# A state-space stage on a clock of TensorE time: eight heads' decay together, Silu on ScalarE, products in column halves

## The chip, the cores and the metric

The kernel runs on one core of one Trainium2 chip. A core has TensorE (PE, matrix products; its weight loads are listed apart as PEld), VectorE (DVE), ScalarE (ACT), GpSimd (POOL) and SyncE (SP, which here only issues transfers). Each engine executes its own list of instructions in order, and semaphores tie the lists together. The metric is device time in microseconds (us) of one execution. 2331.67 us is the median of three runs of the kernel before (2330.33 to 2332.08).

## The reference

Two layers over 256 tokens of width 2048 in float32. The first mixes tokens by attention, the second by a Mamba-2 state-space mixer; each is followed by a dense MLP, and all add to a residual stream. The state-space mixer, cut to what matters (h are the normalised tokens; 8 groups of 8 heads of 64; one chunk of 256 tokens, so the state carried in is zero):

```python
z, xbc, dt = jnp.split(h @ w_in, ...)                    # 4096 | 4096 + 1024 + 1024 | 64 columns
xbc = jax.nn.silu(causal_depthwise_conv(xbc, conv_w, conv_b))   # 4 taps along the tokens
xs, b_in, c_in = jnp.split(xbc, ...)
dt = jax.nn.softplus(dt + dt_bias)
cum = jnp.cumsum(dt * -jnp.exp(a_log))                   # running sum over the tokens
decay = jnp.exp(jnp.where(tril, cum[l] - cum[s], -inf))  # per head, 256 x 256
y = ((c_in @ b_in.T) * decay) @ (xs * dt) + d_skip * xs
y = rms_norm_per_group(y * jax.nn.silu(z)) * norm_g
return y @ w_out
```

## The kernel before, in words

The program is attention, MLP 0, the state-space stage, MLP 1. Float32 weights stream from memory over SP's queue into `wraw` (six buffers). ACT rounds each tile to a high part `wh` (L103), and DVE forms the low part `wl` (L104); each has four buffers, so a new `wh` waits until PE has used the one four units earlier. Such a tile holds two 128-row steps of a 512-column block. PE uses it in twelve matmuls of 128x512: for two steps and two halves of the tokens, activations high by weights high, low by high, and high by low (L326, L327, L330). I call these twelve a unit. The tiles' numbers run through the program; the stage begins with unit 421.

In the stage, a block of eight units projects one of B0, B1, C0, C1, x0 to x7, z0 to z7 (512 columns each) into two `acc` banks of PSUM. `evac` copies the banks to SBUF on ACT (L1090). For B, C and x, `conv` then works in two halves: four PE transposes (L1068), an Identity on ACT (L1074) and three taps on DVE (L1077) for each of two 128-channel tiles, then Silu as Tanh on ACT (L1079) and a product on DVE (L1080). The dt block gives 64 columns. `fold` (L354) turns them to tokens by heads, `dt_chain` computes softplus step by step on DVE (L1107 to L1123, `la` last), and `cums` (L1128, L1129) forms running sums on PE, which go to memory as `cumD` (L1131). `cb_group` makes a group's scores (L1153, L1154).

For an x block, `back` turns the result into tokens by channels (L1176, copied out at L1178), and `across` (L1190, L1192) adds what the first half of the tokens gives to the second. `head` works on one head: it reads its row of `cumD` into every partition (`cm`, L1210), subtracts and clamps on DVE (L1214), takes Exp on ACT (L1215), multiplies by dt and the scores on DVE (L1217), and multiplies on PE (`product`, L1226) into a bank of `yp`. The skip term and `far` are added on POOL and DVE (L1230 to L1233). `z_block` forms Silu of z from Tanh, and `gate` multiplies, normalises (L1264) and turns the result (L311) into operands of the output blocks o0 to o3, which use `acc` banks and end in a residual add on DVE (L396 or L421).

What sets the order: PE's order is the order in which the code issues its instructions. ACT, DVE, POOL and SP are ordered by a scheduler within what the data allows. In the code, small work is put off with `later(n, fn)`, which counts ticks, and a tick comes once in two units; `pump` issues one or two heads at every tick.

Of the kernel before, what the change touches and what calls it, by code (L numbers as in the profile page):

```python
# [43 lines left out]
C_INV, C_DTB, C_ALOG, C_CW, C_CB, C_END = 848, 880, 944, 1008, 1200, 1248  # L44
# [171 lines left out]
class Trunk:  # L216
# [120 lines left out]

    def narrow_block(self, key, tiles, then, lag=1):
# [203 lines left out]
    def mlp_body(self, mp, layer, gain):  # L542
# [47 lines left out]
        def products(accs, key, lhs, kt, first, last):  # L590
            u, (h, lo) = self.flow.next(key)
            for q in range(2):
                k = 2 * kt + q
                wh, wl = h[:, q * 512:(q + 1) * 512], lo[:, q * 512:(q + 1) * 512]
                for t, b in enumerate(accs):
                    ah, al = lhs(k, t)
                    nc.tensor.matmul(b, ah, wh, start=first and q == 0, stop=False)  # L597
                    nc.tensor.matmul(b, ah, wl, start=False, stop=False)  # L598
                    nc.tensor.matmul(b, al, wh, start=False, stop=last and q == 1)  # L599

# [36 lines left out]
        for tok in tokens:  # L637
            key = (tok[0], layer) + tok[1:]
            if tok[0] == "s":
# [8 lines left out]
                products([bank[name]], key, lambda k, t: [x[:, k] for x in S[name]], d,  # L648
# [4 lines left out]
            elif tok[0] == "c":  # L653
# [3 lines left out]
                products(out["c"], key, lhs_x, o, o == 0, o == 7)  # L657
# [8 lines left out]
            else:  # L666
# [3 lines left out]
                products(out[nb], key, lhs_u(p), o, o == 0, o == 3)  # L670
# [364 lines left out]
    def ssm_body(self, sp, dp, gain):  # L1035
        nc, d, cst = self.nc, self.d, self.cst
        xT = self.from_tiles(self.xT)
        rs, rsh = self.rs, self.rsh
        rs2 = self.rs_pool[(self.phase - 1) % 2][:, 0:2]
        tri = sp.tile([P, 256], F32, name="tri")  # L1040
        aneg = sp.tile([P, 64], F32, name="aneg")
        dt = sp.tile([P, 2, 64], F32, name="dt")
        ncum = sp.tile([P, 2, 64], F32, name="ncum")
        edge = sp.tile([P, 2, 64], F32, name="edge")
        cumD = dp.tile([64, S], F32, name="cumD")
        cb = [None] * GROUPS
        fm = {}
        xg = [None] * GROUPS
        yps = {}
        early = [True]  # L1050
        hq, ready, gated = [], set(), set()
        far = [None] * GROUPS

        def setup():
            nc.vector.tensor_copy(tri[:, 0:P], cst[:, C_TRI:C_TRI + P])
            nc.gpsimd.memset(tri[:, P:256], 1.0)
            nc.scalar.activation(aneg, cst[:, C_ALOG:C_ALOG + 64], AF.Exp)

        self.later(0, setup)

        def conv(ev, ct, dst, lag, after):

            def half(j):
                b = self.bank(early[0])
                for k in range(2):
                    for t in range(2):
                        o = k * 256 + t * P
                        nc.tensor.transpose(b[:, o:o + P], ev[t][:, (2 * j + k) * P:(2 * j + k + 1) * P], self.ident)  # L1068
                a = self.scratch()
                for k in range(2):  # L1070
                    c = ct + 2 * j + k
                    wc = lambda i: cst[:, C_CW + 4 * c + i:C_CW + 4 * c + i + 1]
                    s, o = b[:, k * 256:(k + 1) * 256], a[:, k * 256:(k + 1) * 256]
                    nc.scalar.activation(o, s, AF.Identity, bias=cst[:, C_CB + c:C_CB + c + 1], scale=wc(3))  # L1074
                    for i in (2, 1, 0):
                        m = 3 - i
                        nc.vector.scalar_tensor_tensor(o[:, m:256], s[:, 0:256 - m], wc(i), o[:, m:256], ALU.mult, ALU.add)  # L1077
                th = self.scratch()
                nc.scalar.activation(th, a, AF.Tanh, scale=0.5)  # L1079
                nc.vector.scalar_tensor_tensor(dst(j), th, 1.0, a, ALU.add, ALU.mult)  # L1080
# [427 lines left out]
```

## Time and profile before

| what | number |
|---|---|
| median of three runs | 2331.67 us (2330.33 to 2332.08) |
| the profiled execution | 2331.29 us; span of its instructions 2329.5 us |
| PE busy | 2312.2 us |
| DVE, ACT, POOL busy | 1905.8, 1385.4, 205.9 us |
| state-space stage, in the span's time | 961.48 to 1650.25 us |
| TensorE's granted clock | 1.00 |

The span runs from the first instruction to the last; 1.8 us of the execution lie around it. PE carries the time: a microsecond saved elsewhere counts only if PE waited for it. Matmuls overlap each other, so the time one costs is read from the distance between starts and not from its duration. In a row of groups the columns are line, engine, operation, tiles and shapes, count, busy us and mean ns, then the engine's idle time before the group and what ended it; in a timeline row start, busy time, engine, line, operation, tiles, shape and count.

### The profile page before, as it was taken

To read this page: it belongs to the slowest core of one execution; us is meant where nothing else is said; L and a number is where in the kernel's file an instruction comes from. 1 tells how busy PE (TensorE), PEld (TensorE's weight loads), DVE (VectorE), ACT (ScalarE), POOL (GpSimd) and SP (SyncE) were. 2 spreads that over 40 slices of the span, in tenths; PEclk is the share of its full clock that TensorE was granted. 3 is DMA by queue.
4 is the path that set the end of the run, shared out by engine and by line. 5 is a ranking of instruction groups with operands and counts; after the bars stand their busy time and mean duration, and the time that the engine had idled before them with its cause. 6 is when DMAs were issued, how large, how long until landed. Compare 5 with 4: busy or idle time off the path is not lost.

```text
span 2329.5 us, 30294 instructions
## 1 busy us (share of the span) xinstructions
PE 2312.2 (99%) x10799; PEld 1924.8 (83%) x10799; DVE 1905.8 (82%) x2432; ACT 1385.4 (59%) x1869; POOL 205.9 (9%) x239
## 2 busy tenths in 40 slices
PE   9999999999999999999999999999999999999999
PEld 7888888888888888888888888888888888888887
DVE  7776698998899897677788768666888899889885
ACT  6765566566566666555555455445566656666663
POOL 1431000000000000000022101110000000000000
PEclk9999999999999999999999999999999999999999
DMA  8434678878887877666566656656687788788874
GB/s 311 147 121 137 194 226 257 247 246 254 263 242 246 264 215 245 201 202 178 173 191 202 208 187 194 195 176 199 209 254 229 253 264 241 244 269 245 248 229 165
DMA packets 152152, 510.75 MB, mean 219 GB/s; under 512 B 17152, under 2 KB 26304, under 8 KB 152000
## 3 DMA queue, kind: packets, MB, share of 16 engines
q1 hardware_dynamic: 143712, 479.37, 62.6%
q0 software_dynamic: 8064, 29.36, 7.8%
q8 instruction: 85, 1.39, 0.2%
q14 instruction: 67, 0.55, 0.1%
q10 hardware_dynamic: 224, 0.07, 0.0%
HBM read 506.58 MB, written 2.16 MB: 218 GB/s over the span
## 4 chain that ended last, share of the span: by engine, by line
PE 97%; DVE 1%; DMA 1%; ACT 1%; issue 0%; POOL 0%; SPq 0%; DVEq 0%; ACTq 0%; POOLq 0%
PE acc L326 13%; PE acc L327 12%; PE acc L330 12%; PE yp L598 9%; PE yp L599 9%; PE yp L597 9%; PE st L598 8%; PE st L599 8%; PE st L597 8%; PE sm L311 2%; PE y L1226 1%; DVE wl L104 1%; PE acc L597 1%; PE acc L599 1%; PE acc L598 1%; PE acc L706 0%
## 5 line engine op out<-in xcount | busy, mean ns | idle before, releaser
L103 ACT ACTIVATE wh<-wraw 128x1024 fp32r<-128x1024 f32 (+2 forms) x818 | 860.0, 1054 | 633.2 <-PE acc L327 285.4
L104 DVE TENSOR_TENSOR wl<-wraw,wh 128x1024 fp32r<-128x1024 f32 (+2 forms) x818 | 995.3, 1229 | 253.4 <-ACT wh L103 243.7
L597 PE MATMUL yp<-wh,k 128*128 128x512 f32 x896 | 349.9, 390 | 0.0
L598 PE MATMUL yp<-wl,k 128*128 128x512 f32 x896 | 348.9, 389 | 0.6 <-DVE wl L104 0.6
L599 PE MATMUL yp<-wh,k 128*128 128x512 f32 x896 | 348.8, 389 | 0.0
L326 PE MATMUL acc<-wh,xt 128*128 128x512 f32 x704 | 280.5, 398 | 2.1 <-ACT wh L103 2.1
L327 PE MATMUL acc<-wh,xt 128*128 128x512 f32 x704 | 274.8, 390 | 0.0
L103 ACT ACTIVATE wh<-wrx 128x1024 fp32r<-128x1024 f32 x168 | 177.9, 1059 | 135.8 <-PE yp L599 107.5
L104 DVE TENSOR_TENSOR wl<-wrx,wh 128x1024 fp32r<-128x1024 f32 x168 | 203.8, 1218 | 38.2 <-ACT wh L103 38.0
L598 PEld LDWEIGHTS yp<-wl,k 128*128 128x128 f32 x896 | 168.2, 188 | 35.9 <-DVE wl L104 1.4
L326 PE MATMUL acc<-wh,k 128*128 128x512 f32 x496 | 196.8, 397 | 0.6 <-DVE xt L957 0.6
L599 PEld LDWEIGHTS yp<-wh,k 128*128 128x128 f32 x896 | 168.2, 188 | 35.0
L597 PEld LDWEIGHTS yp<-wh,k 128*128 128x128 f32 x896 | 168.2, 188 | 34.6
L327 PE MATMUL acc<-wh,k 128*128 128x512 f32 x496 | 193.4, 390 | 0.0
L330 PE MATMUL acc<-wl,xt 128*128 128x512 f32 x704 | 188.6, 390 | 0.0
L597 PE MATMUL st<-wh,xt 128*128 128x512 f32 x448 | 176.9, 395 | 0.0
L598 PE MATMUL st<-wl,xt 128*128 128x512 f32 x448 | 174.8, 390 | 0.0
L599 PE MATMUL st<-wh,xt 128*128 128x512 f32 x448 | 174.7, 390 | 0.0
L326 PEld LDWEIGHTS acc<-wh,xt 128*128 128x128 f32 x704 | 132.6, 188 | 29.8 <-ACT wh L103 3.7
L330 PEld LDWEIGHTS acc<-wl,xt 128*128 128x128 f32 x704 | 132.1, 188 | 28.2
L327 PEld LDWEIGHTS acc<-wh,xt 128*128 128x128 f32 x704 | 132.7, 188 | 25.9
L200 POOL DMA_DIRECT2D wrx<-mi x56 | 49.0, 875 | 1140.2 <-DVE wl L104 1034.2
(292 smaller groups left out, 3480.8 us busy)
## 6 DMA issues: line engine op xcount, KB each, us to landing
wraw<-mi SPq DMA_DIRECT2D x256, 512.0 KB, 5.1
wraw<-mo SPq DMA_DIRECT2D x256, 512.0 KB, 5.4
wraw<-si SPq DMA_DIRECT2D x160, 512.0 KB, 3.9
wraw<-so SPq DMA_DIRECT2D x64, 512.0 KB, 3.9
wrx<-mi SPq DMA_DIRECT2D x56, 512.0 KB, 5.0
wrx<-mi POOLq DMA_DIRECT2D x56, 512.0 KB, 7.8
wraw<-wo SPq DMA_DIRECT2D x32, 512.0 KB, 3.8
wraw<-ukv SPq DMA_DIRECT2D x16, 512.0 KB, 5.1
```

Source lines behind the costliest of these rows:

```text
L103: self.last = nc.scalar.activation(h[:, v], raw[:, v], AF.Copy)
L104: nc.vector.tensor_tensor(lo[:, v], raw[:, v], h[:, v].bitcast(F32), ALU.subtract)
L200: nc.gpsimd.dma_start(st["b11"].tile, quarter(d, 1, 0), accum_op=ALU.add)
L311: self.nc.tensor.transpose(b[:, j * P:(j + 1) * P], src[:, j * P:(j + 1) * P], self.ident)
L326: nc.tensor.matmul(accs[t][:, :n], ah, wh[:, q, :], start=first and kt + q == 0, stop=False)
L327: nc.tensor.matmul(accs[t][:, :n], al, wh[:, q, :], start=False, stop=False)
L330: nc.tensor.matmul(accs[t][:, :n], lhs(kt + q, t)[0], wl[:, q, :], start=False, stop=en and q == nk - 1)
L597: nc.tensor.matmul(b, ah, wh, start=first and q == 0, stop=False)
L598: nc.tensor.matmul(b, ah, wl, start=False, stop=False)
L599: nc.tensor.matmul(b, al, wh, start=False, stop=last and q == 1)
L1226: nc.tensor.matmul(y[t][:, o], half(t), xg[g][t][:, o], start=True, stop=True)
```

## The change

The stage is rewritten. PE's order now follows a clock (`at`): every unit moves it by 2.72 us, small runs add a fixed charge, and small work is issued when its planned time has come (`when`, `small`, `move`). Blocks come in another order: B0, dt, C0, x0, x1, B1, C1, z0, z1, x2, x3, o0 and so on. Silu is one ACT function in place of Tanh and a DVE product. The decay of a group's eight heads is made in four tiles of 128x512, each holding two heads: four reads of `cumD`, sixteen Relu rows, four Exp rows on ACT, four products with the scores on DVE; dt is multiplied into x (`xd`) instead. A group's product is one run of 32 matmuls, in which each 128x128 stationary tile is split into two halves of 64 columns that write different partitions of the same bank. The skip uses constants, on POOL. The output blocks o0 to o2 accumulate in the two `yp` banks (tiles `so`) instead of in `acc`, and y takes both banks of the pool `sm`, which the transposes and the across results use too. The three products of a weight tile are issued one after another for each bank (`products`).

```diff
-C_INV, C_DTB, C_ALOG, C_CW, C_CB, C_END = 848, 880, 944, 1008, 1200, 1248
+C_INV, C_DTB, C_ALOG, C_CW, C_CB, C_DSK, C_END = 848, 880, 944, 1008, 1200, 1248, 1312
...
+    def products(self, accs, key, lhs, kt, first, last):
+        nc = self.nc
+        u, (h, lo) = self.flow.next(key)
+        for q in range(2):
+            k = 2 * kt + q
+            wh, wl = h[:, q * 512:(q + 1) * 512], lo[:, q * 512:(q + 1) * 512]
+            for t, b in enumerate(accs):
+                ah, al = lhs(k, t)
+                nc.tensor.matmul(b, ah, wh, start=first and q == 0, stop=False)
+                nc.tensor.matmul(b, ah, wl, start=False, stop=False)
+                nc.tensor.matmul(b, al, wh, start=False, stop=last and q == 1)
...
+        at, due = [0.0, 0.0], []
+        count = [0]
+
+        def when(us, fn):
+            count[0] += 1
+            due.append((at[0] + us, count[0], fn))
+
+        def small(us, fn, gap=2.6):
+            at[1] = max(at[0] + us, at[1] + gap)
+            when(at[1] - at[0], fn)
+
+        def move(us):
+            at[0] += us
+            while due and min(due)[0] <= at[0]:
+                e = min(due)
+                due.remove(e)
+                e[2]()
+
...
-                th = self.scratch()
-                nc.scalar.activation(th, a, AF.Tanh, scale=0.5)
-                nc.vector.scalar_tensor_tensor(dst(j), th, 1.0, a, ALU.add, ALU.mult)
-            self.later(lag, lambda: half(0))
-            self.later(lag + 1, lambda: half(1))
-            if after:
-                self.later(lag + 5, after)
...
+                nc.scalar.activation(dst(j, a), a, AF.Silu)
+                if j:
+                    after()
+
+            small(2.5, lambda: half(0))
+            small(2.5, lambda: half(1), 4.0)
...
+            small(3, fold)
...
+                nc.tensor.matmul(b[:64, 0:P], la[:, 0], diagonal(), start=True, stop=True)
+                nc.tensor.matmul(b[:64, P:256], la[:, 0], ones[:, 0:P], start=True, stop=False)
+                nc.tensor.matmul(b[:64, P:256], la[:, 1], diagonal(), start=False, stop=True)
+                at[0] += 0.7
                 nc.scalar.activation(cum, b[:64, 0:256], AF.Copy)
+                nc.scalar.dma_start(cumD.rearrange("a (b s) -> (a b) s", b=2), cum)
+                small(2, back)
...
+            small(8, cums)
...
+            def back(t):
+                b = self.ps(self.sm, "sm")
+                for k in range(4):
+                    o = (k % 2) * 256 + t * P
+                    nc.tensor.transpose(b[:, k * P:(k + 1) * P], fmx[k // 2][:, o:o + P], self.ident)
+                at[0] += 0.45
+                x = sp.tile([P, 512], F32, tag="xtm", name=f"xtm{g}_{t}", bufs=XTM)
+                nc.scalar.activation(x, b, AF.Copy)
+                w = sp.tile([P, 512], F32, tag="xd", name=f"xd{g}_{t}", bufs=XD)
+                nc.vector.tensor_tensor(heads_of(w), heads_of(x), spread(dt[:, t], g), ALU.mult)
+                xg[g][t], xd[g][t] = x, w
+                if t == 0:
+                    xw = self.scratch()
+                    nc.gpsimd.tensor_tensor(heads_of(xw), heads_of(x), spread(edge[:, 0], g), ALU.mult)
+                    small(6, lambda: across(xw))
+                nc.gpsimd.tensor_tensor(heads_of(x), heads_of(x), spread(cst[:, C_DSK:C_DSK + 64], g), ALU.mult)
+                if t:
+                    waiting.append(g)
+                    if len(waiting) == 1:
+                        heads(g)
+
+            def across(xw):
+                b = self.ps(self.sm, "sm")
+                nc.tensor.matmul(b, cb[g][:, 2], xw, start=True, stop=True)
+                at[0] += 0.9
+                far = self.scratch()
+                nc.vector.tensor_tensor(heads_of(far), heads_of(b), spread(edge[:, 1], g), ALU.mult)
+                nc.gpsimd.tensor_tensor(xg[g][1], xg[g][1], far, ALU.add)
+
+            def after():
+                small(7, lambda: back(0))
+                small(7, lambda: back(1))
+
+            conv(ev, 4 * g, dst, after)
...
+        def heads(g):
+
+            cm = []
+            for i in range(4):
+                m = sp.tile([P, 2, 2, P], F32, tag="cm", name=f"cm{g}_{i}", bufs=4)
+                nc.sync.dma_start(m.rearrange("p a t n -> p (a t n)"), cumD[4 * g + i:4 * g + i + 1].to_broadcast([P, 2 * S]))
+                cm.append(m)
+
+            def exponent(i):
+                for k in range(2):
+                    for t in range(2):
+                        h = 8 * g + 2 * i + k
+                        nc.scalar.activation(cm[i][:, k, t], cm[i][:, k, t], AF.Relu, bias=cumT[:, t, h:h + 1], scale=-1.0)
+
+            def decay():
+                for m in cm:
+                    nc.scalar.activation(m, m, AF.Exp, scale=-1.0)
+                scores = cb[g][:, 0:2].rearrange("p t n -> p (t n)").unsqueeze(1).to_broadcast([P, 2, 2 * P])
+                for m in cm:
+                    v = m.rearrange("p a t n -> p a (t n)")
+                    nc.vector.tensor_tensor(v, v, scores, ALU.mult)
+                small(8, product)
+
+            def product():
+                y = [self.ps(self.sm, "y") for t in range(2)]
                 for t in range(2):
+                    for i in range(8):
+                        o = slice(i * 64, (i + 1) * 64)
+                        for r in (slice(0, 64), slice(64, 128)):
+                            nc.tensor.matmul(y[t][r, o], cm[i // 2][:, i % 2, t, r], xd[g][t][:, o], start=True, stop=True)
+                at[0] += 1.8
+                at[1] = max(at[1], at[0])
+                for t in range(2):
+                    nc.vector.tensor_tensor(xg[g][t], xg[g][t], y[t], ALU.add)
+                waiting.pop(0)
+                if waiting:
+                    heads(waiting[0])
+
+                def done():
+                    ready.add(g)
+                    gate(g)
+
+                when(2, done)
+
+            for i in range(4):
+                when(3 + 2.2 * i, lambda i=i: exponent(i))
+            when(11, decay)
...
-            m = sp.tile([P, 256], F32, tag="mt", name=f"mt{h}", bufs=6)
-            half = lambda t: m[:, t * P:(t + 1) * P]
-                nc.vector.tensor_scalar(half(t), cm[:, t * P:(t + 1) * P], ncum[:, t, h:h + 1], 0.0, ALU.add, ALU.min)
-            nc.scalar.activation(m, m, AF.Exp)
-                nc.vector.scalar_tensor_tensor(half(t), half(t), dt[:, t, h:h + 1], cb[g][:, 256 * t:256 * t + P],
-                                               ALU.mult, ALU.mult)
-                    nc.tensor.matmul(y[t][:, o], half(t), xg[g][t][:, o], start=True, stop=True)
-                if i == 7:
-                    for t in range(2):
-                        x = xg[g][t]
-                        nc.gpsimd.tensor_tensor(x, x, dg, ALU.mult)
-                        if t:
-                            nc.gpsimd.tensor_tensor(x, x, far[g], ALU.add)
-                        nc.vector.scalar_tensor_tensor(x, x, 0.5, y[t], ALU.mult, ALU.add)
-                    ready.add(g)
...
+                nc.scalar.activation(w, accs[t], AF.Silu, scale=rs[t])
...
+            small(10, lambda: turn(0))
+            small(10, lambda: turn(1))
+            small(12, lambda: gated.add(g))
...
+                    out = [self.ps(self.yp, "so") for _ in range(2)]
+                self.products(out, ("so", i, nb, o), self.from_tiles(yT_of(yT, i)), o, o == 0, o == 3)
+                if o == 3:
+                    self.add_residual(nb, out)
+                move(2.72)
...
+                self.products(accs, ("si", name, i, o), lhs_x, o, o == 0, o == 7)
+                if o % 2:
+                    self.tick()
+                if o == 7:
+                    done[name](i, accs)
+                move(2.72)
...
-SSM_ORDER = ["x0", "x1", "x2", "z0", "x3", "z1", "x4", "z2", "o0", "x5", "z3", "x6", "z4", "o1",
-             "x7", "z5", "z6", "o2a", "z7", "o2b", "o3"]
+SSM_ORDER = ["B0", "dt0", "C0", "x0", "x1", "B1", "C1", "z0", "z1", "x2", "x3", "o0", "z2", "z3", "x4", "x5", "o1",
+             "z4", "z5", "x6", "x7", "o201", "z6", "z7", "o223"]
```

PE at the end of the block x0, where its transposes stand (`s2` is a scratch tile that an evacuation wrote, `cst` holds the identity). Before (x0's transposes are the four that write `yp_737`):

```order
L330 MATMUL acc_735_9772<-wl463_9728,xt_636_8409 128x512
L330 MATMUL acc_736_9773<-wl463_9728,xt_636_8409 128x512
L1068 MATMUL yp_737_9810<-cst_90,s2_733_9768 128x128
L1068 MATMUL yp_737_9810<-cst_90,s2_734_9770 128x128
L1068 MATMUL yp_737_9810<-cst_90,s2_733_9768 128x128
L1068 MATMUL yp_737_9810<-cst_90,s2_734_9770 128x128
L326 MATMUL acc_735_9772<-wh464_9745,xt_647_8511 128x512
```

and now, units 445 and 446 (`acc_705`, `acc_706` are x0's banks):

```order
L347 MATMUL acc_705_9209<-wl445_9301,xt_669_8715 128x512
L348 MATMUL acc_705_9209<-wh445_9300,xt_670_8716 128x512
L346 MATMUL acc_706_9210<-wh445_9300,xt_669_8715 128x512
L347 MATMUL acc_706_9210<-wl445_9301,xt_669_8715 128x512
L348 MATMUL acc_706_9210<-wh445_9300,xt_670_8716 128x512
L1083 MATMUL sm_715_9402<-cst_90,s2_713_9398 128x128
L1083 MATMUL sm_715_9402<-cst_90,s2_714_9400 128x128
L1083 MATMUL sm_715_9402<-cst_90,s2_713_9398 128x128
L1083 MATMUL sm_715_9402<-cst_90,s2_714_9400 128x128
L346 MATMUL acc_717_9417<-wh446_9325,xt_636_8409 128x512
```

Before, the transposes stood behind the second unit (463) of the next block; now they stand directly behind the last unit of x0, which the evacuations read.

ACT around Silu of an x block's second half and the copies of its transposes back (`xtm`). Before, for x0, whose second Tanh (into `s2_743`) stands seven rows ahead of these, with x1's first half in between:

```order
L103 ACTIVATE wh474_9994<-wraw474_9925 128x1024
L103 ACTIVATE wh475_10030<-wraw475_9943 128x1024
L1074 ACTIVATE s2_752_10015<-sm_751_10010,cst_90 128x256
L103 ACTIVATE wh476_10048<-wraw476_9974 128x1024
L1074 ACTIVATE s2_752_10015<-sm_751_10010,cst_90 128x256
L103 ACTIVATE wh477_10118<-wraw477_9992 128x1024
L1079 ACTIVATE s2_753_10024<-s2_752_10015 128x512
L1178 ACTIVATE xtm0_0_10069<-sm_755_10064 128x512
L1178 ACTIVATE xtm0_1_10076<-sm_756_10071 128x512
```

and now, in x1, whose first transposes back stand on PE behind unit 457:

```order
L103 ACTIVATE wh459_9711<-wraw459_9590 128x1024
L1094 ACTIVATE s2_729_9630<-s2_729_9630 128x512
L1090 ACTIVATE s2_733_9669<-sm_732_9664,cst_90 128x256
L103 ACTIVATE wh460_9729<-wraw460_9642 128x1024
L103 ACTIVATE wh461_9759<-wraw461_9683 128x1024
L1094 ACTIVATE s2_733_9669<-s2_733_9669 128x512
L1214 ACTIVATE xtm1_0_9750<-sm_734_9745 128x512
```

The Silu of the second half (`s2_733`) now stands behind `wh461`, which reuses the buffer of `wh457`, and the transposes back that need it stand right behind unit 457; before, six units' `wh` stood between x0's second Tanh and the copies `xtm0_0`, `xtm0_1`.

DVE at the end of the dt chain. Before:

```order
L104 TENSOR_TENSOR wl438_9132<-wraw438_9075,wh438_9131 128x1024
L1117 SCALAR_TENSOR_TENSOR dt4_9051<-dt4_9051,dt3_9050 128x128 x4
L104 TENSOR_TENSOR wl439_9150<-wraw439_9093,wh439_9149 128x1024
L1117 SCALAR_TENSOR_TENSOR dt4_9051<-dt4_9051,dt3_9050 128x128 x3
L1118 SCALAR_TENSOR_TENSOR dt4_9051<-dt4_9051,dt2_9049 128x128
L1120 SCALAR_TENSOR_TENSOR dt_8757<-dt4_9051,dt0_9047 128x128
L1123 SCALAR_TENSOR_TENSOR la_9071<-dt_8757,aneg_8756 128x64 x2
L104 TENSOR_TENSOR wl440_9168<-wraw440_9111,wh440_9167 128x1024
```

and now, with `s2_694` and `s2_695` as scratch tiles of the chain and `la` in the last row:

```order
L1162 SCALAR_TENSOR_TENSOR s2_694_9020<-s2_694_9020 128x128
L104 TENSOR_TENSOR wl436_9086<-wraw436_8999,wh436_9085 128x1024
L1162 SCALAR_TENSOR_TENSOR s2_694_9020<-s2_694_9020 128x128
L104 TENSOR_TENSOR wl437_9110<-wraw437_9047,wh437_9109 128x1024
L1162 SCALAR_TENSOR_TENSOR s2_694_9020<-s2_694_9020 128x128
L1163 SCALAR_TENSOR_TENSOR s2_694_9020<-s2_694_9020,s2_695_9023 128x128
L1165 SCALAR_TENSOR_TENSOR dt_8755<-s2_694_9020 128x128
L1167 SCALAR_TENSOR_TENSOR s2_695_9023<-dt_8755,s2_695_9023 128x64 x2
```

The chain now shares DVE with a `wl` at each step, the last of them `wl437`; on PE the running sums stand behind unit 433.

More of the change, by code (lines that the diff above doesn't have):

```diff
@@ L1036, in ssm_body @@
         nc, d, cst = self.nc, self.d, self.cst
[L1037 to L1041, printed above, removed]
+        lhs_x = self.from_tiles(self.xT)
+        xT, rs = self.xT, self.rs
         dt = sp.tile([P, 2, 64], F32, name="dt")
-        ncum = sp.tile([P, 2, 64], F32, name="ncum")
+        cumT = sp.tile([P, 2, 64], F32, name="cumT")
@@ L1044, in ssm_body @@
         edge = sp.tile([P, 2, 64], F32, name="edge")
[L1045 to L1057, printed above, removed]
@@ new lines, in cb_group @@
+        def cb_group(g):
+            B, C = fm["B", g // 4][:, g % 4], fm["C", g // 4][:, g % 4]
+            b = self.ps(self.sm, "sm")
+            nc.tensor.matmul(b[:, 0:256], B[:, 0:P], C, start=True, stop=True)
+            nc.tensor.matmul(b[:, 256:384], B[:, P:256], C[:, P:256], start=True, stop=True)
+            at[0] += 0.65
+            t = sp.tile([P, 3, P], F32, name=f"cb{g}")
+            for i in range(2):
+                nc.vector.tensor_tensor(t[:, i], b[:, 2 * i * P:2 * i * P + P], diagonal(), ALU.mult)
+            nc.scalar.activation(t[:, 2], b[:, P:256], AF.Copy)
+            cb[g] = t
@@ new lines, in dt_products, with fold @@
+        def dt_products():
+            w = [t.rearrange("p (k n) -> p k n", n=P) for t in self.flow.next(("si", "dt", 0, 0))[1]]
+            acc = self.ps(self.sm, "sm")
+            for kt in range(16):
+                for i in range(2):
+                    nc.tensor.matmul(acc[:, :256], w[kt // 8][:, kt % 8], xT[kt // 4][i][:, kt % 4],
+                                     start=kt == 0 and i == 0, stop=kt == 15 and i == 1)
+            v = self.scratch()
+            nc.vector.tensor_copy(v[:, :256], acc[:, :256])
+            def fold():
+                b = self.ps(self.sm, "sm")
+                for t in range(2):
+                    nc.tensor.matmul(b[:, t * 64:(t + 1) * 64], v[:, t * P:(t + 1) * P], cst[:, C_SEL:C_SEL + 64],
+                                     start=True, stop=True)
+                dt_chain(b)
+            small(3, fold)
@@ L1104, in dt_chain @@
         def dt_chain(b):
-            v, e, s, z, q = (sp.tile([P, 2, 64], F32, name=f"dt{i}") for i in range(5))
+            work = self.scratch()
+            v, e, z, q = (work[:, i * P:(i + 1) * P].rearrange("p (t h) -> p t h", t=2) for i in range(4))
             for t in range(2):
@@ new lines, in ssm_body @@
+        while due:
+            assert at[0] < 1e6
+            move(max(0.0, min(due)[0] - at[0]))
+        assert len(gated) == GROUPS
+        self.boundary_begin(gain, True)
+        for pair in ((0, 1), (2, 3)):
+            accs = {}
+            for nb in pair:
+                accs[nb] = self.block([("so", 6, nb)], self.from_tiles(yT_of(yT, 3)), last=False)
+            for nb in pair:
+                self.block([("so", 7, nb)], self.from_tiles([yT[7]]), accs=accs[nb], first=False)
+                self.finalize(nb, accs[nb], False)
@@ L1488 @@
     a["sng"] = rows(f(ssm_norm_g)[0], 512)
-    a["dsk"] = rows(np.repeat(f(ssm_d)[0], 64), 512)
     one = np.ones((P, P), np.float32)
```

297 lines of the change are left out of this document (118 added, 179 removed).

## The prediction

> **What bounds the kernel now.** I read the page's table of engines first, then the state-space stage alone (from the first projection matmul to the last of o3's), then the waits of TensorE (PE).
>
> ```profile
> span 2329.5 us, 30294 instructions
> ...
> PE 2312.2 (99%) x10799; PEld 1924.8 (83%) x10799; DVE 1905.8 (82%) x2432; ACT 1385.4 (59%) x1869; POOL 205.9 (9%) x239
> ...
> 961.48:1650.25 688.77, 687.76 (x3294) 571.62 (x3292) 509.53 (x822) 362.84 (x503) 84.16 (x68) 1.00 0.62 192
> ...
> PE sm L1068 <- ACT xtm L1178: 0.5, 1, 0.5
> ...
> PE sm L1176 <- DVE s L1077: 0.2, 1, 0.2
> ```
>
> PE is busy 99% of the span. In the stage it is busy 687.76 of 688.77 us (second and third number of the row; then PE's weight loads, DVE, ACT, POOL, the clock at 1.00 and the DMA). So it stands idle for 1.0 us, and its small matmuls wait twice. VectorE (DVE, 509.53) and ScalarE (ACT, 362.84) have room. Only two things can move the time: less work on PE, or new waits in PE's fixed order. A faster helper engine alone buys 1.0 us at most.
>
> What PE's small runs cost is the distance between starts:
>
> ```profile
> 1110.93 1.07 PE L330 MATMUL acc<-wl,xt 128*128 128x512 f32 x4
> 1111.84 0.60 PE L1068 MATMUL sm<-cst,s 128*128 128x128 f32 x4
> 1112.19 0.48 PE L326 MATMUL acc<-wh,xt 128*128 128x512 f32 x1
> 1112.51 0.39 PE L327 MATMUL acc<-wh,xt 128*128 128x512 f32 x1
> ...
> 1132.12 1.02 PE L1190 MATMUL sm<-s,cb 128*128 128x512 f32 x2
> 1132.98 1.00 PE L1226 MATMUL y<-xtm,mt 128*128 128x64 f32 x8
> 1133.79 0.48 PE L326 MATMUL acc<-wh,xt 128*128 128x512 f32 x1
> 1134.11 0.39 PE L327 MATMUL acc<-wh,xt 128*128 128x512 f32 x1
> ...
> L1226 PE MATMUL y<-xtm,mt 128*128 128x64 f32 x256 | 33.5, 264 | 0.0
> ```
>
> Four big matmuls take 0.91 us from start to start (1110.93 to 1111.84), so 0.227 us each and 2.72 for a weight unit of twelve. A matmul runs 0.39 us, so it ends 0.16 us after its slot. Four transposes put 0.35 us in front of the next matmul and 0.09 behind it (0.32 to the next start instead of 0.23): 0.44. Two heads' products, 8 records, cost 0.81 + 0.09 = 0.90. The 256 records are 32 such pairs: 28.7 us.
>
> **The change, part by part.** Column halves first. Now 64 records stand together per group, each with 64 stationary columns and a 64-wide stream. No row shows two column tiles at work. The nearest is the running sums, which use one tile of 64 columns:
>
> ```profile
> 994.31 0.56 PE L354 MATMUL sm<-cst,s 128*128 128x64 f32 x4
> ...
> 1010.23 1.07 PE L330 MATMUL acc<-wl,xt 128*128 128x512 f32 x4
> 1011.22 0.65 PE L1128 MATMUL sm<-tri,la 128*64 128x256 f32 x2
> 1011.71 0.38 PE L1129 MATMUL sm<-tri,la 128*64 128x128 f32 x2
> 1012.02 0.50 PE L326 MATMUL acc<-wh,xt 128*128 128x512 f32 x1
> ...
> 1011.22 0.19 PEld L1128 LDWEIGHTS sm<-tri,la 128*64 128x64 f32 x2 [0.35 <-issue]
> 1011.49 0.35 PEld L1129 LDWEIGHTS sm<-tri,la 128*64 128x64 f32 x2
> ```
>
> After 1010.23 the next start was due 0.91 later, at 1011.14; it came at 1011.22, so entering and leaving the 64-column form costs about 0.2 us together. A record of the old product takes 0.101 us (0.81 over 8). With half the columns I put 0.056, half of the same spacing with its surcharge (0.90 over 8 is 0.112). One after the other, 64 records take 3.6 + 0.2 = 3.8 us a group: 30.4 in all, a loss of 1.7. If both halves work at once, 1.8 + 0.2 = 2.0: 16 in all, a gain of 12.7. If loads did not hide behind matmuls, 64 x 0.11 + 0.2 = 7.2: 57.6, a loss of 28.9. I take 2.0, at six to four against 3.8: the halves write different partitions and hold their own weights. The clock in the code charges 1.8 here, and its other charges (0.45 for four transposes, 0.9 across) agree with the rows (0.44; 1132.12 to 1132.98).
>
> On this row bears a rule against the change: the Trainium skill, "TensorE: Matmul & The Clock Gate", Part 3, says that a weight load overlaps matmuls in flight only when its row group differs. Both halves use all rows, so by it the sum would take 57.6. The trace disagrees: L1129's loads began at 1011.49, while L1128's matmuls ran to 1011.87, in the same rows. The same skill's "TensorEngine Tiling (Array Packing)", Tiling Modes, has different tiles load and multiply in parallel, which gives the 16; no run here shows it yet.
>
> Next, PE's waits. The clock in `move` runs small work at a planned time, but a block's last unit is charged only after its evacuation was booked, so `small(2.5)` lands directly behind that unit. PE executes in order and stands there. Prices:
>
> ```profile
> L1090 ACT ACTIVATE s<-acc,rs 128x512 f32<-128x512 f32 x24 | 15.0, 674 | 0.0
> L103 ACT ACTIVATE wh<-wraw 128x1024 fp32r<-128x1024 f32 x225 | 238.3, 1060 | 255.6 <-PE acc L327 210.8 <-issue 24.8 <-DVE mt L1214 6.9
> L1079 ACT ACTIVATE s<-s 128x512 f32<-128x512 f32 x24 | 15.1, 631 | 4.7 <-DVE s L1077 4.1
> ...
> L104 DVE TENSOR_TENSOR wl<-wraw,wh 128x1024 fp32r<-128x1024 f32 x225 | 282.8, 1261 | 128.1 <-ACT wh L103 126.8
> L421 DVE TENSOR_TENSOR x<-acc,x 128x512 f32<-128x512 f32 x24 | 15.4, 684 | 9.1 <-PE acc L330 9.1
> L1117 DVE SCALAR_TENSOR_TENSOR dt<-dt,dt 128x128 f32<-128x128 f32 x7 | 2.0, 289 | 0.2
> L1123 DVE SCALAR_TENSOR_TENSOR la<-dt,aneg 128x64 f32<-128x64 f32 x2 | 0.4, 222 | 0.0
> ...
> 1112.48 0.57 ACT L1074 ACTIVATE s<-sm,cst 128x256 f32<-128x256 f32 x1 [0.24 <-PE sm L1068]
> ...
> 1012.53 0.37 ACT L1130 ACTIVATE cum<-sm 64x256 f32<-64x256 f32 x1
> 1012.93 0.50 ACTq L1131 DMA_DIRECT2D cumD<-cum  x1
> 1017.37 0.81 SPq L1210 DMA_DIRECT2D cm<-cumD  x2
> ...
> L1109 ACT ACTIVATE dt<-dt 128x128 f32<-128x128 f32 x1 | 0.3, 288 | 0.0
> ...
> DMA to landing us min/median/max: 2.9/3.6/4.9
> ```
>
> From PE's end to ACT's start is 0.04 us (1111.84 + 0.60 to 1112.48); back to PE I put 0.05.
>
> 1. *Transposes behind a block's end.* The second bank's evacuation starts 0.16 + 0.04 after the unit and takes 0.67, plus 0.05: 0.92. The first bank's transpose runs in the first 0.1 of it, so 0.82 is lost, at six blocks (B0, x0, C1, x2, x4, x6): 4.9. B1 is a little later (1.0). In x1, x3, x5, x7 the across matmul stands ahead and covers all but 0.1: 0.4. At C0, ACT has twelve Relu rows and two wh ahead of the second evacuation, and the Relus wait for the running sums' round trip: copy 0.4, write 4.4 (1012.93 to the first read at 1017.37), read 3.6, Relus of 0.2 to 0.29 each, 2 x 1.06, 2 x 0.67 are 14.3 to 15.3 us after the sums, and C0 ends 11.3 after them (four units and a small run): 3 to 4, I take 3.0, since such rows overlap. Sum 9.3.
> 2. *Running sums.* `la` stands on DVE behind wl437, that behind wh437, which reuses the buffer of unit 433, the unit just finished: 0.2 + 1.06 + 1.26 + three DVE steps of 0.29 + two of 0.22 + 0.05 = 3.9, say 4.0. Before, 17 us of other matmuls lay between fold and sums (994.31 to 1011.22).
> 3. *B0's second half* wants the bank that DVE's copy of the dt product empties: 0.7.
> 4. *Odd x groups (x1, x3, x5, x7), first transposes back.* The second Silu stands on ACT behind the wh that reuses the buffer of the unit just finished: 0.2 + 1.06 + 0.63 + 0.05 = 1.9, less 0.2 for the two transposes that can go: 1.75 x 4 = 7.0.
> 5. *Across behind the product (same groups).* Its bank is y's of the even group, freed by a DVE add that stands behind a wl, behind a wh, behind the last big matmul: 0.2 + 1.06 + 1.26 + 0.68 = 3.2 against 2.0 of product: 1.15 x 4 = 4.6. With the product at 3.8 this is nothing.
> 6. *o blocks.* They accumulate in two banks of `yp` instead of four of `acc`, so a new column block waits for the residual add. The add of the first bank can start 0.5 before the unit ends and takes 0.68: 0.26; with one wl ahead about 0.6. At five places (two in o0, two in o1, one in o2): 2.9; the others fall under case 4.
>
> Sum of the waits: 9.3 + 4.0 + 0.7 + 7.0 + 4.6 + 2.9 = 28.5 us. The 1.0 us of old idle time goes.
>
> At nothing I cost what has cover. DVE loses the per-head work (L1214, L1217) and Tanh's second half. ACT gets 17 more table loads, 1.28 us each (22 us), and 128 Relu rows of 0.29 at most (37):
>
> ```profile
> L438 ACT ACT_TABLE_LOAD x1 | 1.3, 1283 | 1.2 <-PEq L1501 1.2
> ...
> L1214 DVE TENSOR_SCALAR mt<-cm,ncum 128x128 f32<-128x128 f32 x128 | 37.8, 338 | 0.0
> L1217 DVE SCALAR_TENSOR_TENSOR mt<-mt,dt,cb 128x128 f32<-128x128 f32 x128 | 39.5, 349 | 2.6 <-ACT mt L1215 2.3
> ```
>
> ACT then has some 420 of 700 us. A wh is made three units (8.2 us) ahead of its use, so two table loads in its way stay hidden; without that lead each would cost 1.3. The skip moves to POOL, off PE's path; gate chains get three units and need about 7 us. On SP's queue the four reads of a group's decay tiles now wait for the previous product, and weights stand behind them, but the next weight needs a buffer that frees no earlier: nothing.
>
> Sum: 2331.29 - 12.7 - 1.0 + 28.5 = 2346.1 us. The profiled execution (span 2329.5 plus 1.8 around it) is 0.4 below the median of the runs, 2331.67; that is inside the 0.2% (5 us) which I take as no change. I say 2346.
>
> **The rivals.**
> - *Halves one after the other* (0.25). The running sums' loads of one tile speak for it. Product -12.7 becomes +1.7, case 5 vanishes: 2331.3 + 1.7 - 1.0 + 23.9 = 2356.
> - *Loads not hidden* (0.05): the product adds 28.9, case 5 vanishes: 2331.3 + 28.9 - 1.0 + 23.9 = 2383. The overlap at 1011.49 speaks against it.
> - *Faster* (0.18): the other side. The halves overlap, and ACT and DVE take their ready short rows in time, so that PE's waits stay under the 13.7 us that the product and the old idle time give. The place is cases 2, 4 and 5, where the rows stand behind a wh that needs the unit just done. It decides at 13.7 us, about half of my waits; at a third (9.5) the time is 2327. Against it: engines run their rows in order in this trace (PE stood 0.49 us at L1068 for L1178), and the rows do stand so.
> - *No net change* (0.10): waits of 9 to 18 us, 2327 to 2336.
>
> **How the numbers follow.** My forecast (0.42) gives 2346, and 2339 to 2352 by case 1 at C0 and case 6 between their floors (0.8 and 0.26) and twice their price, with half a microsecond of lateness at each long wait. The range reaches down into the faster rival, 2326, and up past the serial one with the same lateness, 2362. Below lies most of the faster case, above the unhidden loads. Faster by over 0.2%: 0.18; within 0.2%: 0.10; slower: 0.72.
>
> **What would show it.** In the profile after: records of the product 28 ns apart (or 56, or 110); a wait of PE's transposes for the evacuation, about 0.8 us a dozen times in all; one of about 4 us for `la`; four near 1.75 for Silu; four near 1.1 for the y add; PE idle near 28 us where it was 1.0. I am wrong if PE's idle time in the stage stays under 14 us, or if the products take 3.8 a group.

## The result, and the profile after

The changed kernel takes 2353.9 us (median of four runs, 2352.72 to 2357.35) against 2331.43: 22.5 us more, a ratio of 1.0098 [1.0086, 1.011]. Its profiled execution took 2352.72 us. The head of its page, and the stage as a stretch of time (us, then busy us and instructions of PE, its weight loads, DVE, ACT, POOL, then clock, DMA share and GB/s):

```profile
span 2350.9 us, 30618 instructions
```

```profile
960.99:1671.17 710.18, 684.69 (x3551) 558.95 (x3550) 449.23 (x565) 410.55 (x617) 75.38 (x69) 1.00 0.58 183
```

PE's waits in the stage (what waited, for what; total us, times, longest):

```profile
PE sm L1083 <- ACT s L1072: 5.8, 11, 1.8
PE sm L1211 <- ACT s L1094: 5.8, 4, 1.4
...
PE sm L1175 <- DVE s L1167: 4.5, 1, 4.5
PE sm L1230 <- DVE xtm L1275: 4.3, 4, 1.1
PE so L346 <- DVE x L433: 4.0, 4, 1.7
...
PE sm L1083 <- DVE s L1133: 0.5, 1, 0.5
```

The span grew by 21.4 us, and so did the stage (710.18 against 688.77): the rest of the span kept its length to 0.1 us. PE now stands idle for 25.5 us of it (710.18 less 684.69) where it was 1.0, and the six waits listed, 24.9 us, are nearly all of that. L1083 are the transposes behind a block, L1211 the transposes back, L1175 the running sums, L1230 the across matmul, L346 into `so` the first matmul of an output column block.

The product of a group (timeline: start, busy us, engine, line, operation, tiles, shape, count):

```profile
1118.85 0.39 PE L348 MATMUL acc<-wh,xt 128*128 128x512 f32 x1
1119.17 2.08 PE L1271 MATMUL y<-xd,cm 128*64 128x64 f32 x64
1121.19 0.50 PE L346 MATMUL acc<-wh,xt 128*128 128x512 f32 x1
1121.52 0.39 PE L347 MATMUL acc<-wl,xt 128*128 128x512 f32 x1
```

The 64 records follow each other in 2.02 us (1119.17 to 1121.19), 32 ns each, where a full record took 101 before and the prediction put 56 for halves one after the other. The two halves work at once. With 0.09 in front (1118.85 + 0.23 to 1119.17) and 0.10 behind (0.33 to the next start) a group costs 2.2 us, all eight 17.7 instead of 28.7.

The longest wait, and what it did to the clock. First the rows around it:

```profile
1001.15 0.39 PE L348 MATMUL acc<-wh,xt 128*128 128x512 f32 x1
1001.57 1.06 ACT L103 ACTIVATE wh<-wraw 128x1024 fp32r<-128x1024 f32 x1 [0.24 <-PE acc L348]
...
1002.26 1.22 DVE L104 TENSOR_TENSOR wl<-wraw,wh 128x1024 fp32r<-128x1024 f32 x1
1003.40 0.28 DVE L1162 SCALAR_TENSOR_TENSOR s<-s 128x128 f32<-128x128 f32 x1
1003.60 1.22 DVE L104 TENSOR_TENSOR wl<-wraw,wh 128x1024 fp32r<-128x1024 f32 x1
1004.74 0.28 DVE L1162 SCALAR_TENSOR_TENSOR s<-s 128x128 f32<-128x128 f32 x1
...
1005.71 0.36 DVE L1167 SCALAR_TENSOR_TENSOR s<-dt,s 128x64 f32<-128x64 f32 x2
1005.99 0.69 PE L1175 MATMUL sm<-cst,s 128*64 128x128 f32 x2 [4.45 <-DVE s L1167]
...
1009.76 0.63 PE L348 MATMUL acc<-wh,xt 128*128 128x512 f32 x1
1010.18 0.63 PE L346 MATMUL acc<-wh,xt 128*128 128x512 f32 x1
```

and stretches of time, with PE's busy time as the second number and the granted clock as the third from the end:

```profile
1002.00:1005.00 3.00, 0.00 (x0) 0.00 (x0) 3.00 (x6) 0.63 (x1) 0.00 (x0) 1.00 0.82 259
1005.00:1012.00 7.00, 6.01 (x17) 4.78 (x18) 0.97 (x5) 0.38 (x1) 0.00 (x0) 0.51 0.58 197
1012.00:1014.00 2.00, 2.00 (x12) 1.39 (x11) 0.81 (x4) 1.45 (x2) 0.00 (x0) 1.00 0.73 158
```

The rows that were predicted are there: the last big matmul ends, ScalarE (ACT) rounds the weights of unit 437 (1001.57 to 1002.63), VectorE (DVE) makes their low part (1003.60) and only then the last steps of `la`. But DVE did not wait for this rounding. It was still making the low part of the unit before (1002.26), and the row of 1002 to 1005 has it busy for 3.00 of 3.00 us; its list has no gap from 996.6 until `la` is done. So the length of DVE's own list set the wait, and not the buffer that the unit just ended gave free. Then PE runs at half clock until 1012: big matmuls start 0.42 us apart instead of 0.227. Some 6 us of work at half speed lose 3 us.

The sum of 21.4 us: idle time +24.5; about 25 waits in which the first 0.16 us still count as busy, since the matmul before them is draining, +4.0; half clock +3.0; products -11.0; 0.9 not assigned.

### The profile page after: what moved, and what is told of

Same layout as the page of the kernel before. It is cut to its first block, busy times and chain, and to the rows that moved or that the text cites. A ratio compares the mean times of both kernels' runs of the same rounds, so it can differ in the third digit from the quotient of the medians.

```text
span 2350.9 us, 30618 instructions
## 1 busy us (share of the span) xinstructions
PE 2310.1 (98%) x11057; PEld 1913.3 (81%) x11057; DVE 1846.3 (79%) x2174; ACT 1432.9 (61%) x1982; POOL 196.4 (8%) x239
## 4 chain that ended last, share of the span: by engine, by line
PE 92%; DVE 2%; DMA 2%; ACT 2%; issue 1%; POOL 0%; SPq 0%; DVEq 0%; ACTq 0%
PE yp L347 9%; PE yp L348 9%; PE yp L346 9%; PE st L347 7%; PE st L348 7%; PE st L346 7%; PE acc L346 6%; PE acc L348 6%; PE acc L347 6%; PE acc L326 5%; PE acc L327 4%; PE acc L330 4%; PE so L346 2%; PE so L348 2%; PE so L347 2%; PE sm L311 1%
## 5 line engine op out<-in xcount | busy, mean ns | idle before, releaser
L346 PE MATMUL yp<-wh,k 128*128 128x512 f32 x896 | 349.8, 390 | 0.0
L346 PE MATMUL acc<-wh,xt 128*128 128x512 f32 x704 | 280.9, 399 | 0.5 <-DVE x L408 0.5
L347 PE MATMUL acc<-wl,xt 128*128 128x512 f32 x704 | 274.8, 390 | 0.0
L346 PEld LDWEIGHTS yp<-wh,k 128*128 128x128 f32 x896 | 168.2, 188 | 34.6
L346 PE MATMUL st<-wh,xt 128*128 128x512 f32 x448 | 176.8, 395 | 0.0
L348 PEld LDWEIGHTS acc<-wh,xt 128*128 128x128 f32 x704 | 132.6, 188 | 28.5
L346 PEld LDWEIGHTS acc<-wh,xt 128*128 128x128 f32 x704 | 132.8, 189 | 27.2 <-DVE x L408 0.9
L346 PE MATMUL st<-wh,sN 128*128 128x512 f32 x336 | 132.3, 394 | 0.0
L348 PE MATMUL st<-wh,sN 128*128 128x512 f32 x336 | 130.9, 390 | 0.0
```

## Experiments

Each was timed in three rounds against the kernel before, whose median lay between 2331.2 and 2331.8. "Changed kernel" is the one of the prediction.

**1. Full columns.**

```diff
-                        for r in (slice(0, 64), slice(64, 128)):
-                            nc.tensor.matmul(y[t][r, o], cm[i // 2][:, i % 2, t, r], xd[g][t][:, o], start=True, stop=True)
+                        nc.tensor.matmul(y[t][:, o], cm[i // 2][:, i % 2, t], xd[g][t][:, o], start=True, stop=True)
```

> The changed kernel with one edit: each 128x128 tile of a group's product is one matmul again instead of two halves of 64 columns. Theory (the halves work at once: 2.2 us a group in the changed kernel, and the across matmul behind it waits about 1.1 us for y's bank): the product goes back to about 3.6 us a group, +11 us over eight groups, and the four waits of the across matmuls (4.3 us of idle time) vanish: about +6, 2360 us. Rival (the halves run one after the other, and the records only overlap on paper): no change, 2354 us within 1.

2355.25 us, ratio 1.0103 [1.0087, 1.012]: 1.4 above the changed kernel, which is inside the spread of its runs, and neither forecast. By the time alone the rival (no change) comes nearer. The waits tell more:

```profile
PE sm L1083 <- ACT s L1072: 4.0, 12, 0.5
PE so L346 <- DVE x L433: 2.4, 4, 0.9
```

L1230 no longer waits, as expected; L1083 and `so` wait 3.4 us less in sum. A longer product gives the helper engines time, so most of its price was hidden under waits. The half clock behind `la` also lasted for 3.41 us here and for 6.83 in the changed kernel. Experiment 8 repeats the edit where there are no waits.

**2. Sums later.** `small(8, cums)` becomes `small(13.5, cums)`.

> The changed kernel with one edit: the running sums are issued two units later (13.5 instead of 8 us on the clock). Theory (the 4.5 us wait for la makes TensorE's clock fall to half for the next 6 us): the wait and the half-clock stretch both go, 4.5 + 2.7, so -7 us, 2347 us, and the granted clock is 1.00 throughout. Rival 1 (the half clock is not tied to the wait): -4.5 us, and a stretch of half clock stays somewhere. Rival 2 (another operation takes the wait over, the reads of the decay tiles being two units later): the time stays at 2354 with a new wait at C0's transposes.

2348.27 us (2344.54 to 2351.66), ratio 1.0072 [1.0057, 1.0087]: 5.6 less. The wait for `la` fell from 4.5 to 0.5, and the half clock behind it went. But another stretch of half clock appeared at a place where the changed kernel had none:

```profile
1122.29:1125.71 3.42, 1.63 (x9) 0.94 (x9) 1.92 (x2) 3.42 (x7) 0.00 (x0) 1.00 0.54 163
1125.71:1129.12 3.41, 3.41 (x10) 2.65 (x9) 2.58 (x4) 2.74 (x9) 0.00 (x0) 0.50 0.66 198
```

It follows 3.42 us in which PE was busy for 1.63. The measured time lies between the theory's and that of rival 1, which had a stretch of half clock stay somewhere. Which light stretch is followed by half clock differs between kernels whose rows there are alike; the last section has what decides. It may also be behind the spread of up to 7 us between executions of one kernel, but of each kernel only one execution has a trace.

**3. Conv later**, and **4. Back later.**

```diff
-            small(2.5, lambda: half(0))
-            small(2.5, lambda: half(1), 4.0)
+            small(5.2, lambda: half(0))
+            small(5.2, lambda: half(1), 4.0)
```

```diff
-                small(7, lambda: back(0))
-                small(7, lambda: back(1))
+                small(9.7, lambda: back(0))
+                small(9.7, lambda: back(1))
```

> The changed kernel with one edit: the transposes behind a block's end are issued one unit later (5.2 instead of 2.5 us on the clock). Theory (they wait for an evacuation that starts only when the block has ended): their idle time of 5.8 us goes, and with the end of the last matmul that overlaps it, 0.16 each, some 8 us: 2346 us. Rival (whatever follows a block is on a chain as long as the wait, and the wait moves to Silu and the transposes back): less than 3 us gained, with L1211 waiting longer.

> The changed kernel with one edit: the transposes back of x are issued one unit later (9.7 instead of 7 us on the clock). Theory (in odd groups they wait for a Silu that stands on ScalarE behind a rounding of weights which needs the unit just ended): the four waits of 1.4 us go, 5.8 of idle time and 6.7 with what overlaps: 2347 us. Rival (the wait is for Silu itself, which is late by more than a unit): the waits stay, 2354 us.

2352.06 us, ratio 1.0089 [1.0074, 1.0104], and 2353.47 us, ratio 1.0097 [1.0082, 1.0112]: next to nothing. In each the wait aimed at went (L1083 for L1072 from 5.8 to 0.2; L1211 from 5.8 to none), and others took its place. PE's waits of experiment 3, then of 4:

```profile
PE so L346 <- DVE x L433: 8.4, 5, 3.1
...
PE sm L1175 <- DVE s L1167: 5.1, 1, 5.1
PE y L1271 <- DVE s L1093: 4.3, 1, 4.3
```

```profile
PE so L346 <- DVE x L433: 6.1, 4, 2.1
...
PE y L1271 <- DVE cm L1262: 1.8, 1, 1.8
```

In 3 the taps (L1093) come later, and a product and the residual adds meet them; four stretches of half clock instead of one add the rest. The rivals' outcome came true, though not by the way they named: the wait did not move to Silu but to the o blocks and the product.

**5. o in acc** (`self.acc_tile()` instead of `self.ps(self.yp, "so")`), and **6. Across apart**:

```diff
                 small(8, product)
+                at[1] += 2.72
```

> The changed kernel with one edit: the output blocks o0 to o2 accumulate in the acc banks again instead of the two yp banks. Theory (with two banks a column block waits for the residual add of the one before): the waits of so behind x's add, 4.0 us, go, with 0.16 of overlap each: -4.6, 2349 us. Rival (the wait goes on to the next operation of the chain, as in the runs with one lag moved): less than 2 us gained.

> The changed kernel with one edit: after a product the next small run is planned a unit later, so that across no longer stands directly behind the product. Theory (across waits for y's bank, which a VectorE add frees late): the four waits of 1.1 us go, -4 to -5 us, 2349 us. Rival (everything behind the product is a unit later and pays it back at the gate or the o blocks): 2354 us.

2349.44 us, ratio 1.0076 [1.006, 1.0093], and 2349.2 us, ratio 1.0081 [1.0066, 1.0096]: -4.5 and -4.7, as the theory had it. In the profile of 6 the waits of `across` are gone and the others stay within 1 us. In that of 5 the waits of `so` are gone, but L1083 waits for 7.5 us instead of 5.8, and the stage has three stretches of half clock of 3.41 us instead of one of 6.83; with runs of one kernel some 5 us apart, it is partly luck that the time meets the forecast.

**7. All five lags** (2 to 6 together).

> The five edits together: sums two units later, transposes behind a block and transposes back a unit later, across apart from the product, o blocks in the acc banks. Theory (the waits add up, and each goes if what it waits for gets one more unit and the banks allow it): 24 us of idle time and the half clock go, and the product's gain of 11 us is left: 2331.5 - 11 to - 8, 2320 to 2324 us, with a clock of 1.00. Rival (helper chains are as long as the distances, so that waits move on, as in the runs with one lag moved, which gained 0 and 2 us instead of 7 and 8): 2340 us or more.

2321.43 us (2320.12 to 2322.96), ratio 0.9959 [0.9944, 0.9974]: faster than both kernels. One by one the five edits bring 5.6 + 1.8 + 0.4 + 4.5 + 4.7 = 17 us, together 32. The single gains are uncertain by some 3 us each, but the traces say the same: PE's waits in the stage, 24.9 us in the changed kernel, are 19.8, 23.1, 24.2, 22.6 and 20.3 us in experiments 2 to 6, so that they fall by 14.5 us in sum, and by 23.7 when the edits stand together. The stage in its profile, and the only waits left in it:

```profile
961.93:1639.70 677.77, 676.53 (x3551) 558.01 (x3550) 451.31 (x565) 411.47 (x619) 77.02 (x69) 1.00 0.61 192
```

```profile
PE sm L1175 <- DVE s L1167: 0.8, 1, 0.8
...
PE sm L1116 <- ACT cb L1122: 0.4, 1, 0.4
```

PE is idle for 1.2 us, about as in the kernel before, and its busy time is 11.2 us lower (676.53 against 687.76).

**8. All lags, full columns** (edit 1 on top of 7).

> The kernel with all five lags (2321.4 us), with the product in full columns again. Theory (its lead over the kernel before is the column halves' and nothing else's): the product goes from 2.2 to about 3.6 us a group, 8 x 1.4 = 11 us: 2332 us, the same as the kernel before, and still no wait. Rival (halves are worth less, and the rest comes from the batched decay or Silu, which took work off the helper engines): 2325 us or less.

2330.99 us, ratio 0.9996 [0.9987, 1.0006]: the kernel before's time (2331.79 in the same rounds) within a microsecond.

```profile
1113.12 3.68 PE L1271 MATMUL y<-xd,cm 128*128 128x64 f32 x32
1116.61 0.48 PE L346 MATMUL acc<-wh,xt 128*128 128x512 f32 x1
```

A group takes 3.5 us from 1113.12 to 1116.61, without a wait. The column halves, worth 9.6 us here (2330.99 against 2321.43), are the whole gain of the change. The batched decay, Silu on ACT and the skip by constants together cost or bring no more than the interval leaves (-3.0 to +1.4 us); one by one they were not tested.

**9 and 10. All lags, but the sums at 8, and at 10.8.**

> The kernel with all five lags, with the running sums back at 8 us on the clock, two units earlier. Theory (one wait of over 4 us also halves TensorE's clock for 3.5 or 7 us): 4.5 + 1.8 or 3.5, so 2327.5 to 2329.5 us, one stretch of half clock in the profile, right behind the wait. Rival (the half clock comes from the small runs with their light load, not from standing still): +4.5 without a stretch of half clock, 2326 us.

> The same with the running sums at 10.8 us, one unit earlier than in the kernel with all lags. Theory: the wait is about 4.5 - 2.7 = 1.8 us, 2 us at most with a late queue; such a wait was followed by half clock in some runs and not in others (1.5 us in one, 1.7 and 1.5 without), so +2 without, +4 with: 2323 to 2325.5 us. Rival (only long waits halve the clock): exactly the wait, 2323.3 us, and a clock of 1.00.

2328.97 us, ratio 0.9988 [0.9978, 0.9997], and 2327.59 us, ratio 0.9981 [0.9972, 0.999]. Against experiment 7 that is +7.5 and +6.2. The wait and the clock in 9, then the wait in 10:

```profile
PE sm L1175 <- DVE s L1167: 5.1, 1, 5.1
```

```profile
1005.97:1012.80 6.83, 3.92 (x12) 3.11 (x13) 2.85 (x9) 0.38 (x1) 0.00 (x0) 0.50 0.70 236
```

```profile
PE sm L1175 <- DVE s L1167: 3.5, 1, 3.5
```

In 9 the wait grew by 4.3 us, and half clock sets in while PE still stands: 6.83 us of it, in which PE was busy for 3.92 and so lost 2.0. The time is the theory's, but not all of it comes from this wait: the scores (L1116, 1.4) and a product (0.4) wait too, so that PE's waits are 6.9 us in all, 5.7 more than in experiment 7. With the 2.0 that makes 7.7, against 7.5 measured. In 10 I was off: one unit later shortens the wait by 1.6, not 2.7, since DVE's order moves with it (four low parts stand among the last dt steps, in 9 three). A product (1.3) and the scores (1.1) wait too, and 3.41 us of half clock stand behind the wait for `la`: 4.7 more of waits and 1.7 of clock, against 6.2 measured. What a wait of under 2 us does to the clock, which this run was meant to show, it does not test.

**11. All lags, but two banks for o.**

> The kernel with all five lags, with o0 to o2 accumulating in the two yp banks again. Theory (with two banks each column block waits for the residual add, which stands on VectorE behind the weights' low parts and the convolution's taps): 4 to 8 us of waits at the starts of column blocks, 2326 to 2330 us. Rival (with the other lags right, VectorE reaches the adds in time): under 2 us, 2323 us.

2338.1 us, ratio 1.0026 [1.0016, 1.0036]: +16.7 to experiment 7, twice what I expected.

```profile
PE so L346 <- DVE x L433: 11.1, 7, 2.2
```

With the other lags set right these waits are longer than in the changed kernel (4.0 us). Why, no run separates: there, other waits may have given the residual adds time, or the longer lags put other work before the adds on DVE. The scores wait for 1.7 us in this profile, and 3.41 us of half clock stand behind one of the waits of `so`. The rival (DVE reaches the adds in time) falls.

**12. Reads early.** Eight `cm` tiles instead of four, read from `back(0)` on:

```diff
-            cm = []
-            for i in range(4):
-                m = sp.tile([P, 2, 2, P], F32, tag="cm", name=f"cm{g}_{i}", bufs=4)
...
+            cm = read.pop(g)
...
+                if t == 0:
+                    reads(g)
```

> The changed kernel with one edit: eight decay tiles instead of four, read when a group's x is turned back, so that the reads no longer wait for the product of the group before. Theory (in the changed kernel ScalarE stands 31 us in its own queue before Relu rows whose tiles have not landed, and the weights' roundings and evacuations behind them are late): this idle time goes but for the first group, the waits at B1 and C1 fall from 1.8 and 2.5 to 0.9, those of the o blocks from 4.0 to about 2.5: -4, 2350 us. Rival (ScalarE has enough lead, and the reads cost nothing): 2354 us within 1.

2363.55 us, ratio 1.014 [1.0124, 1.0157]: the slowest of all, and no test of what I meant. ACT's groups in the stage, of the changed kernel and of this one:

```profile
L1254 ACT ACTIVATE cm<-cm,cumT 128x128 f32<-128x128 f32 x128 | 40.3, 389 | 31.1 <-DMA cm<-cumD 31.1
```

```profile
L1260 ACT ACTIVATE cm<-cm,cumT 128x128 f32<-128x128 f32 x128 | 40.7, 389 | 28.1 <-DMA cm<-cumD 27.6 <-PE so L348 0.4
```

The scheduler used the earlier reads to put the Relu rows of a later group where the earlier group's had stood, right behind a read again: the second group's 16 rows moved from 1098 to 1033 us, and the third's took their place. ACT stood for 27.6 us, 3.5 less than before. PE's waits in the stage rose from 24.9 to 28.5 us (L1083 from 5.8 to 8.1), and the stage has three stretches of half clock, 10.2 us in all instead of 6.8. In experiment 7 it also stands 31.6 us for these reads, and PE does not wait; so the standing alone is not the cost. What the reads cost where distances are short stays open.

## Why the prediction was right, point by point

The forecast was slower, 2346 in a range of 2326 to 2362; measured were 2353.9. The order of ACT's and DVE's rows, with durations from the trace of before, named the place of every wait that came. Its steps, with 0.16 us added to each wait measured, for the drain:

| step | predicted | measured |
|---|---|---|
| product | 2.0 a group, -12.7 | 2.2 a group, -11.0 |
| 1 and 3, transposes behind blocks, dt's bank | 10.0 | 8.2 |
| 2, running sums | 4.0 | 4.6 |
| 4, transposes back | 7.0 | 6.4 |
| 5, across behind the product | 4.6 | 4.9 |
| 6, output blocks | 2.9 | 4.6 |
| waits together | 28.5 | 28.7 |
| half clock | none | +3.0 |

That the waits agree to 0.2 us in sum is luck, since the steps are off by up to 1.8 us to both sides. The forecast rise is 14.8 us; between the profiled executions the span rose by 21.4. The difference of 6.6 is 1.7 of the product, 1.0 of idle time (24.5 + 4.0 against 28.5 - 1.0), 3.0 of half clock and the 0.9 not assigned. The profiled execution is the fastest of the four, 1.2 below their median.

- *Column halves.* Right: 32 ns a record against the forecast's 28. Of the Trainium skill's two rules that the prediction weighed, "TensorEngine Tiling (Array Packing)", Tiling Modes (tiles load and multiply in parallel), agrees with these 2.02 us for 64 records; by the other, from "TensorE: Matmul & The Clock Gate", Part 3, they would have taken 7. The rival of halves one after the other, whose time of 2356 the measurement lies nearest, is false: the time came near it for another reason.
- *Case 1* came near in sum (8.2 for 10.0) and was wrong in places. C0 waited 0.5 instead of 3.0, and C1 2.1 instead of 0.8. ACT stood before Relu rows whose tiles were read only after the previous product:

```profile
1125.15 0.99 ACT L1254 ACTIVATE cm<-cm,cumT 128x128 f32<-128x128 f32 x3 [4.24 <-DMA cm<-cumD]
...
1130.76 1.24 ACT L1072 ACTIVATE s<-acc,rs 128x512 f32<-128x512 f32 x2
1131.48 0.33 PE L1083 MATMUL sm<-cst,s 128*128 128x128 f32 x1 [1.84 <-ACT s L1072]
```

- *Case 2* came near (4.6 for 4.0) by another path than the one it added up. It let DVE stand until the rounding of unit 437 was done; the rows show DVE at work without a gap, with one more low part before that of 437. So the wait was as long as DVE's list up to `la`, though nothing in that list stood waiting.
- *At nothing I cost what has cover.* Partly false in the changed kernel. I counted ACT's load (420 us predicted, 410.55 measured) but not that these reads stop its queue for 4 us at a time; a Relu row took 0.39 us, not 0.29. That the batched decay, Silu and the skip in sum cost nothing in a kernel without waits is shown by experiment 8. That a late ACT made C1 and the o blocks wait is read from rows like those above; no run separated it.
- *Case 6* was too small: waits of 1.5 and 1.7 us at the starts of two column blocks, where a `wl` that was late behind ACT stood before the add.
- *The term that failed* is one that was not in the sum: a price that a wait has on PE's clock. It is 3.0 us of the 6.6 that the forecast lacks, and in experiment 9 it is 2.0 us on top of the waits.
- *The rival "faster"* said that it decides at 13.7 us of waits. Without them (experiment 7) the kernel gains 9.8 us on the kernel before (2331.2 to 2321.4), near the sum without waits: 2331.3 - 11.0 - 1.0 = 2319.3.

## What to carry to other kernels

When PE's order is written by a clock, charge a unit before booking what follows it, and check each small run against the queue of the engine it waits for: a short operation behind a weight rounding that needs the unit just ended is as late as that unit plus the rounding. Waits of this kind do not add up one by one: here five edits bring 17 us singly and 32 together, so they are mended together, and a part of the change (the column halves) is judged in a kernel without waits. A bank saved at one place can cost more than a good part of the change brings: two instead of four for the output blocks cost 16.7 us in experiment 11, the column halves bring 9.6.

## What the runs showed of the hardware

- *Half clock after idle time.* After the 4.5 us wait PE's granted clock was 0.5 for 6.83 us; in eight experiments single stretches of 3.41 us appeared in the stage. The Trainium skill, "TensorE: Matmul & The Clock Gate", Part 1, tells of a gate with two states and a free-running window of 3.4 us, and the stretches agree with one or two such windows. It gives about one idle window as what closes the gate; in experiment 2 a stretch followed 3.42 us in which PE was still busy for 1.63.

The traces show more. In every profile with more than one half-clock stretch (in each profile one begins within 1.6 us of the program's end) their starts lie whole multiples of 3.413 us apart, so each execution can be cut into cells of 3.41 us on that grid. The changed kernel around `la`, and then at C1's transposes (PE's busy time is the second number, the clock the third from the end):

```profile
1001.59:1005.00 3.41, 0.00 (x0) 0.00 (x0) 3.41 (x6) 1.04 (x1) 0.00 (x0) 1.00 0.75 238
1005.00:1008.41 3.41, 2.42 (x8) 1.98 (x9) 0.97 (x5) 0.38 (x1) 0.00 (x0) 0.50 0.97 329
1008.41:1011.83 3.42, 3.42 (x9) 2.67 (x8) 0.00 (x0) 0.00 (x0) 0.00 (x0) 0.50 0.23 74
1011.83:1015.24 3.41, 3.41 (x17) 2.55 (x16) 1.83 (x5) 2.68 (x5) 0.00 (x0) 1.00 0.80 234
...
1127.88:1131.29 3.41, 1.76 (x8) 1.13 (x6) 2.15 (x3) 3.40 (x6) 0.00 (x0) 1.00 0.48 166
1131.29:1134.71 3.42, 2.99 (x14) 2.40 (x15) 1.93 (x4) 3.42 (x9) 0.00 (x0) 1.00 0.57 158
```

Over the stage in all 14 profiles, 17 cells at full clock had PE busy for less than 1.45 us, and half clock followed each of them; 2909 had it busy for more than 1.70 us, and it followed none. Of three between, the cell with 1.50 us kept the clock, and those with 1.63 and 1.66 lost it. After a cell at half clock the full clock came back where PE had been busy for 3.07 us or more (19 cells), and did not where it had been busy for 2.43 or less (5 cells). Where the grid lies differs from execution to execution, so the same wait falls into one cell or is shared by two: the 1.7 us that the changed kernel stood at an output block were split (PE busy for 2.26 and 2.81 us of the two cells), and its clock stayed.
- *Two column halves at once.* A 64-column record with its own weight load costs 32 ns against 109 for a full one (3.49 us for 32 in experiment 8): per product 1.7 times as fast, not twice, at any rate for a stream of 64.
